# A decoder step with sparse attention and pooling: the pooling means in a queue of their own, and the order of the projections

## The chip, the core and the metric

The kernel runs on one core of a Trainium2 chip. The core has five engines with instruction streams of their own: PE (matrix products and transposes, into PSUM), DVE, ACT and POOL (element-wise work; POOL reads no PSUM here), and SP, which only issues transfers. The metric is the device time of one execution in microseconds, median of three.

## The reference, cut to what matters

One layer of a decoder for 1024 prompt tokens and 8 samples with one token each, 1024 channels. One projection feeds an attention that is cut to 256 keys by an indexer, and a pooling mixer.

```
h = rms_norm(x, norm_w) * (1 + scale) + shift
q, k, v, qi, ki, wi, ga, u, gp = split(h @ w_in)
q, k = rms_norm(q, q_norm_w), rms_norm(k, k_norm_w)          # per head of 64
score = sum over 8 heads of wi * relu(qi . ki)               # causal
sel   = the 256 largest scores of a token
a_out = attention of q over k[sel], v[sel] * silu(ga)        # 8 heads, 2 key heads
d[g]  = mean of u[g] over the last w tokens - u[g]           # w = 2, 4, 8, 16 for groups 0..3
p_out = (d[g] @ w_pool[g]) * pool_scale * silu(gp)
y     = x + gate * (concat(a_out, p_out) @ w_out)
```

For the samples the same runs over 1024 cached keys, values and indexer keys in pages. Returned are y, the new k, v and ki, and the last 15 rows of u for prompt and samples.

## The kernel before, in words

Tokens lie along the free dimension (1032 = 1024 prompt + 8 samples), channels on the 128 partitions. Every product is made of three passes over a split into an upper and a lower part (L514); splits take a copy on ACT and a subtraction on POOL. A projection of 128 columns (`project`, L520) goes through three chunks of 344 tokens (two of 388 for qi), 24 matmuls per partial sum of eight channel blocks, 72 in all.

PE, DVE and ACT run in the order in which the program issues (`manual_schedule`, L424). That order is made by a tick: after every two channel blocks, six matmuls, `project` calls `tick` (L169). It runs what the last chunk left to consume, and then takes one step of each of several queues of generators (`beside`, L155): a queue has a list of generators, of which only the first advances, and a rate; a rate of 1.0 is one step per tick, `SCORE` 0.62 a step in about 1.6 ticks, `TOP` 0.5 one in two. `lag(n)` lets n steps pass without work, and so puts distance between two operations. `drain` (L194) issues what is left in named queues without projections between. POOL's instructions and SP's transfers are ordered by the scheduler, not by the ticks.

First half (`first_order`, L1095): k, the indexer queries qi1 to qi3, gates ga0 to ga2 and v. Beside them run `indexer_keys` and `norm_keys` (queue "prep"; L1043), and in "score" `indexer` (L655), 48 units: matmuls `pi` (L668), a relu on ACT (L670) and a weighted sum on DVE (L677). Then "score" is drained (L1150).

Second half (`order`, L1096): pooling inputs u0 to u3, pooling gates gp0 to gp3, queries q0 to q3 and the gate ga3. Beside them run:

- "prep": `values`, `history`, then `windows(g, u)` (L1180) after each u, and the norms of each q (`take_q`, L1239), one after the other;
- "smp": `sample_indexer` (L868), a pipeline over the eight samples with a period of `IXP` steps (load, transposes `pkin`, copy `kidT`, product `p_ix`, copy `sx`, transposes `p_ixT`, weighing `rx`), then `sample_topk` (L936), a binary search of twelve counts in which DVE makes flags `s_fl` (L968), PE sums them (`p_cnt`, L954) and DVE takes the next step (L972 to L976);
- "top": `topk` (L738): eight halvings of a threshold for blocks 2 to 7, with three sign passes on ACT (L758) and three counts on DVE (L761) each, then `tk_keep`, `tk_d`, `tk_t` (L764 to L768); after these the marking of the largest scores;
- "pool": the pooling product and gate (`take_gp`, L1212), which reads `pooled[g]`;
- "gate" (`gate_rows`, L1493) and "stack" (`stack_k`, `stack_q`), which prepare the output gate and the attention's operands; they start with gp3 and q3, the tenth and the twelfth of 13.

`windows` makes log2(w) shifted sums on POOL (L1187), the mean minus u on DVE (L1192 to L1197), its upper part `pdh` on ACT one step later (L1201), the lower part `pdl` on POOL (L1202), and last it transposes the final rows of u (`put`, L1204) for the output.

The norms of a query group take squares summed on PE (`pqs`), a copy `qs` (L1252), transposes (`pqt`), a reciprocal root that begins with a power on POOL (L253), and DVE's steps, which end in `rq8` and in `qbd` (L1265, L1266), the scaled queries of the samples. The attention over the prompt and the samples' attention (`sample_attention`, L1278) come after the drain at L1539; the samples' first product `p_sl` (L1303) reads `qbd` of all four groups. The output projection ends the kernel.

Large tiles (128 x 1032) come from a pool "rows" of 29 buffers (L98).

Of the kernel before, what the change touches and what calls it, by code (L numbers as in the profile page):

```python
# [21 lines left out]
TOP = 0.5  # L22
SCORE = 0.62
BLOCKS = (3, 4, 2, 5, 7, 6)
ILAG = 1
ILAG0 = 3
QLAG = 3
GLAG = 3
IXP = 4
IXB = 13  # L30
LAG = 5
# [34 lines left out]
def kernel(  # L66
# [40 lines left out]
    def row(name, dt=F32, n=N):  # L107
        return rows.tile([P, n], dt, tag="row", name=name)
# [759 lines left out]
    def sample_indexer():  # L868
# [60 lines left out]

        yield from pipeline(B, IXP, (0, load), (5, turn), (6, copy), (8, dot), (9, copy_x), (IXB, back), (IXB + 1, weigh))  # L930

# [111 lines left out]
    def norm_keys():  # L1043
# [15 lines left out]
        nc.sync.dma_start(k_prompt.rearrange("(b p) d -> p b d", p=P), khat.rearrange("p (b d) -> p b d", d=P))  # L1059
        yield  # L1060
        for g in range(2):
# [118 lines left out]
    def windows(g, u):  # L1180

        w = POOL_WINDOWS[g]
        cur = u
        d = 1
        while d < w:
            nxt = row(f"ps{g}_{d}")
            nc.gpsimd.tensor_tensor(nxt[:, d:S], cur[:, d:S], cur[:, 0:S - d], op=ALU.add)  # L1187
            nc.gpsimd.tensor_copy(nxt[:, 0:d], cur[:, 0:d])
            cur = nxt
            d *= 2  # L1190
            yield from lag(3)
        nc.vector.tensor_tensor(cur[:, S:N], hsum[:, g, :], u[:, S:N], op=ALU.add)  # L1192
        head = small.tile([P, HIST], F32, tag="phead", name=f"ph{g}")[:, 0:w - 1]
        nc.vector.tensor_tensor(head, cur[:, 0:w - 1], inv15[:, 0:w - 1], op=ALU.mult)
        nc.vector.scalar_tensor_tensor(cur[:, w - 1:N], cur[:, w - 1:N], 1.0 / w, u[:, w - 1:N],
                                       op0=ALU.mult, op1=ALU.subtract)
        nc.vector.tensor_tensor(cur[:, 0:w - 1], head, u[:, 0:w - 1], op=ALU.subtract)  # L1197
        hi, lo = row(f"pdh{g}", F32R), row(f"pdl{g}", F32R)
        pooled[g] = (hi, lo)
        yield  # L1200
        nc.scalar.copy(hi, cur)  # L1201
        nc.gpsimd.tensor_tensor(lo, cur, hi.bitcast(F32), op=ALU.subtract)  # L1202
        pt = ps_two(f"put{g}", (HIST + B, P))
        nc.tensor.transpose(pt, u[:, S - HIST:N], ident)  # L1204
        yield
        nc.scalar.copy(up_out[:, g * P:(g + 1) * P], pt)
        if g == 3:
            yield
            nc.sync.dma_start(pool_prompt, up_out[0:HIST, :])
            nc.sync.dma_start(pool_sample[:, HIST - 1, :], up_out[HIST:HIST + B, :])  # L1210

    def take_gp(g):  # L1212
# [26 lines left out]
    def take_q(j):  # L1239
# [3 lines left out]
        def norms():  # L1243
# [276 lines left out]
    for o, name in enumerate(order):  # L1520
        beside("weights", next_weights(len(first_order) + o), 1.0)
        i = int(name[-1])
        kind = name[:-1]
        if name == "gp3":
            beside("gate", gate_rows(), 1.0)
        if name == "q3":
            beside("stack", stack_k(), 1.0)
            beside("stack", stack_q(0), 1.0)
        if kind == "u":
            u = row(f"u{i}")  # L1530
            project(name, CHUNKS, copy_out(u))
            beside("prep", windows(i, u), 1.0)
        elif kind == "gp":
# [3 lines left out]
        else:  # L1537
            project(name, CHUNKS, take_ga(i))
    drain("prep", "pool", "top", "smp", "stack")  # L1539
    in_order.close()  # L1540
# [222 lines left out]
```

## Time and profile before

| | |
|---|---|
| time, median of 3 runs | 644.74 us (644.22 to 647.06) |
| the profiled execution | 646.98 us, span 645.3 us |
| mean clock granted to PE | 0.983 of full speed |
| instructions | 10974 |
| PE / DVE / ACT / POOL busy | 606.9 / 409.8 / 291.5 / 234.1 us |
| HBM read, written | 54.44 MB, 11.10 MB |

Times in the profile are counted from the first instruction of the span. "Idle before" is how long the engine had stood still before an instruction, and behind the arrow stands what released it. PE's first projection of the second half (u0) starts at 184.08 us, its last (ga3) ends at about 385; the attention goes on to about 546, the output projection to the end. The profile counts matmuls as busy with modelled ends, so two that overlap, or one that is followed at once, leave no gap.

### The profile page before, as it was taken

To read this page: it belongs to the slowest core of one execution; us is meant where nothing else is said; L and a number is where in the kernel's file an instruction comes from. 1 tells how busy PE (TensorE), PEld (TensorE's weight loads), DVE (VectorE), ACT (ScalarE), POOL (GpSimd) and SP (SyncE) were. 2 spreads that over 40 slices of the span, in tenths; PEclk is the share of its full clock that TensorE was granted. 3 is DMA by queue.
4 is the path that set the end of the run, shared out by engine and by line. 5 is a ranking of instruction groups with operands and counts; after the bars stand their busy time and mean duration, and the time that the engine had idled before them with its cause. 6 is when DMAs were issued, how large, how long until landed. Compare 5 with 4: busy or idle time off the path is not lost.

```text
span 645.3 us, 10974 instructions
## 1 busy us (share of the span) xinstructions
PE 606.9 (94%) x4197; PEld 500.2 (78%) x4197; DVE 409.8 (64%) x950; ACT 291.5 (45%) x518; POOL 234.1 (36%) x205
## 2 busy tenths in 40 slices
PE   5899998999989987988999998999999999999997
PEld 4678988999979877977989885656675666878876
DVE  4797365736467779997785546565677755454242
ACT  5635444444447865231223445755687545302000
POOL 3202434111267555552633591610445143106000
PEclk9999999999999988997999998999999999999999
DMA  8994115031335122121354350420221036146331
GB/s 302 287 272 95 50 44 152 14 88 54 76 114 161 34 66 56 45 57 44 80 128 156 99 164 27 138 99 34 66 67 34 1 99 218 46 157 205 99 98 68
DMA packets 75292, 66.05 MB, mean 102 GB/s; under 512 B 21828, under 2 KB 63900, under 8 KB 75229
## 3 DMA queue, kind: packets, MB, share of 16 engines
q1 hardware_dynamic: 69731, 50.57, 27.6%
q0 software_dynamic: 3008, 10.49, 5.4%
q10 hardware_dynamic: 2498, 4.27, 1.8%
q8 instruction: 33, 0.54, 0.3%
q14 instruction: 22, 0.18, 0.1%
HBM read 54.44 MB, written 11.10 MB: 102 GB/s over the span
## 4 chain that ended last, share of the span: by engine, by line
PE 73%; DVE 13%; ACT 5%; DMA 3%; SPq 2%; POOL 2%; issue 2%; ACTq 0%; POOLq 0%; DVEq 0%
PE py L1696 14%; PE po L1612 7%; PE pj_q L514 6%; PE pT L1596 6%; PE pl L1575 6%; PE pj_ga L514 6%; PE pj_qi L514 4%; PE pj_gp L514 4%; ACT sg L758 4%; PE pi L668 4%; PE pj_k L514 2%; PE pj_v L514 2%; DVE tk_t L768 2%; PE pj_u L514 2%; PE pj_ki L568 2%
## 5 line engine op out<-in xcount | busy, mean ns | idle before, releaser
L1584 ACT ACTIVATE pr<-pr,mx,rq 128x128 f32<-128x128 f32 (+7 forms) x64 | 55.5, 868 | 17.4 <-DVE mx L1582 17.0
L677 DVE SCALAR_TENSOR_TENSOR sc<-r,wtok,sc 128x512 f32<-128x512 f32 (+5 forms) x42 | 44.0, 1059 | 28.1 <-ACT r L670 26.8
L670 ACT ACTIVATE r<-pi 128x512 f32<-128x512 f32 (+5 forms) x48 | 36.3, 760 | 54.2 <-PE pi L668 41.0
L1612 PE MATMUL po<-pTs,v_sb 128*64 128x256 f32 (+1 forms) x320 | 52.6, 381 | 0.0
L1696 PE MATMUL py<-woh,mh 128*128 128x512 f32 (+1 forms) x136 | 52.1, 383 | 0.0
L1696 PE MATMUL py<-wol,mh 128*128 128x512 f32 (+1 forms) x136 | 51.8, 381 | 0.0
L1696 PE MATMUL py<-woh,ml 128*128 128x512 f32 (+1 forms) x136 | 51.8, 381 | 0.0
L1596 PE MATMUL pT<-ident,pr 128*128 128x128 f32 x288 | 48.8, 283 | 0.1
L1578 DVE CUSTOM_DVE_ANT_0 pr<-pl,amask 128x384 f32<-128x384 f32 (+5 forms) x48 | 42.2, 886 | 9.9 <-PE pl L1575 9.5
L1596 PEld LDWEIGHTS pT<-ident,pr 128*128 128x128 f32 x288 | 32.6, 141 | 17.6 <-issue 15.6
L1716 DVE TENSOR_TENSOR y<-py,gate_p 128x512 f32<-128x512 f32 (+1 forms) x17 | 11.2, 658 | 43.0 <-PE py L1696 42.9
L145 ACT COPY pTs<-pT 128x512 f32<-128x512 f32 x40 | 23.3, 582 | 33.5 <-PE pT L1596 33.5
L514 PE MATMUL pj_u<-hh,wh_u 128*128 128x344 f32 x96 | 32.9, 343 | 1.6 <-ACT r L670 1.6
L514 PE MATMUL pj_gp<-hh,wh_gp 128*128 128x344 f32 x96 | 33.2, 346 | 0.0
L514 PE MATMUL pj_q<-hh,wh_q 128*128 128x344 f32 x96 | 33.0, 344 | 0.0
L147 DVE COPY pTs<-pT 128x512 f32<-128x512 f32 (+1 forms) x40 | 23.3, 582 | 15.0 <-PE pT L1596 12.3
L1440 POOL TENSOR_TENSOR wol<-wo,woh 128x1024 fp32r<-128x1024 f32 x8 | 19.5, 2442 | 36.5 <-ACT woh L1439 29.7
L514 PE MATMUL pj_q<-hl,wh_q 128*128 128x344 f32 x96 | 31.6, 330 | 0.0
L514 PE MATMUL pj_gp<-hl,wh_gp 128*128 128x344 f32 x96 | 31.6, 329 | 0.0
L514 PE MATMUL pj_q<-hh,wl_q 128*128 128x344 f32 x96 | 31.6, 329 | 0.0
L514 PE MATMUL pj_gp<-hh,wl_gp 128*128 128x344 f32 x96 | 31.5, 328 | 0.0
L1612 PEld LDWEIGHTS po<-pTs,v_sb 128*64 128x64 f32 x320 | 18.0, 135 | 17.4 <-issue 9.6
(451 smaller groups left out, 1766.2 us busy)
## 6 DMA issues: line engine op xcount, KB each, us to landing
ada<-in_w_ada_dram SPq DMA_DIRECT2D x16, 512.0 KB, 6.9
x<-in_x_prompt_dram SPq DMA_DIRECT2D x8, 512.0 KB, 5.6
gate<-in_w_ada_dram SPq DMA_DIRECT2D x8, 512.0 KB, 3.5
mix<-mix_dram SPq DMA_DIRECT2D x8, 512.0 KB, 3.1
xr<-in_x_prompt_dram SPq DMA_DIRECT2D x15, 256.0 KB
out_dram<-y ACTq DMA_DIRECT2D x15, 256.0 KB, 3.4
mix_dram<-sga SPq DMA_DIRECT2D x12, 172.0 KB, 5.0
mix_dram<-sgp SPq DMA_DIRECT2D x12, 172.0 KB, 2.7
```

The lines of the kernel that those rows point to most:

```text
L145: nc.scalar.copy(out, in_)
L514: mm(pt[:m, :n], wt[:, k, :m], ht[k][:, c0:c0 + n], start=k == 0 and q == 0, stop=k == KT - 1 and q == 2)
L668: mm(pt[:, c, :n], lhs, kk[:, l0:l0 + n], start=kk is kih, stop=kk is kil)
L670: nc.scalar.activation(r[:, 0:L].rearrange("p (c n) -> p c n", c=nh), pt[:, 0:nh, :n], AF.Relu)
L677: nc.vector.scalar_tensor_tensor(sb[:, 0:L], r[:, 0:L], wtok[:, b, h:h + 1], sb[:, 0:L], op0=ALU.mult, op1=ALU.add)
L758: nc.scalar.activation(junk_tile("sg", tag="junka", bufs=1)[:, :L], score[b], AF.Sign, scale=-1.0, bias=t[:, i:i + 1], accum_out=cnt[:, i: ...
L1575: mm(pt[:, c, :n], qst[j][s][:, b * P:(b + 1) * P], ksst[s][w][:, l0:l0 + n], start=w == 0, stop=w == 1)
L1578: nc.vector.tensor_tensor_reduce(out=pr[:, 0:L].rearrange("p (c n) -> p c n", c=nh), in0=pt[:, 0:nh, :n], in1=amask[b].rearrange("p (c n) ...
L1584: exps.append(lambda: nc.scalar.activation(pr[:, 0:L], pr[:, 0:L], AF.Exp, scale=sc, bias=mx, accum_out=sums[j, m][:, bq, s:s + 1]))
L1596: nc.tensor.transpose(pt[:, s, bq * P:(bq + 1) * P], probs[j, 2 * m + bq, s][:, k * P:(k + 1) * P], ident)
L1612: mm(po[j, m][64 * s:64 * s + 64, 0, q0:], v_sb[:, k, 64 * s:64 * s + 64], pTs[j, m, k][:, s, q0:], start=k == 0, stop=k == nk - 1)
L1696: mm(pt[:, part], a[k][:, bs], w[:, part], start=k == ks[0] and q == 0, stop=k == ks[-1] and q == 2)
```

## The change

`windows` goes from the queue "prep" to a new queue "win", which is created later and so comes after "smp" and "top" in a tick. In it the `put` transposes come first, two steps after the projection, and the means last: two further steps (`WLAG - 1`) behind the three of the last sum, then three steps (`WLAG`) to `pdh` and one to `pdl`; `pooled[g]` is set after that. The order of the projections ends in q2, q3, gp3, ga3 instead of gp3, q2, q3, ga3; "gate" and "stack" start at the same places in the count. `SCORE` is 0.68. In the samples' pipeline `p_ix` comes one step later, `sx` and `p_ixT` two, `rx` two. `norm_keys` waits three steps instead of one before its second transposes. The copy `qs` is on ACT.

```
--- before.py
+++ after.py
@@ -20,14 +20,15 @@
 AHEAD = 1
 HOP = 3
 TOP = 0.5
-SCORE = 0.62
+SCORE = 0.68
 BLOCKS = (3, 4, 2, 5, 7, 6)
 ILAG = 1
 ILAG0 = 3
 QLAG = 3
+WLAG = 3
 GLAG = 3
 IXP = 4
-IXB = 13
+IXB = 15
 LAG = 5
 SMP = 1.2
 
@@ -927,7 +928,7 @@
                 op0=ALU.max, op1=ALU.mult)
             nc.vector.tensor_reduce(out=s_sc[:, 0:8, b], in_=rx[b], axis=AX.X, op=ALU.add)
 
-        yield from pipeline(B, IXP, (0, load), (5, turn), (6, copy), (8, dot), (9, copy_x), (IXB, back), (IXB + 1, weigh))
+        yield from pipeline(B, IXP, (0, load), (5, turn), (6, copy), (9, dot), (11, copy_x), (IXB, back), (IXB + 1, weigh))
 
     steps = const.tile([P, 7, B], F32, name="steps")
     nc.gpsimd.iota(steps, pattern=[[1, 7], [0, B]], base=1, channel_multiplier=0,
@@ -1057,7 +1058,7 @@
             yield
             yield from norm_k(pt, khat[:, g * 512:(g + 1) * 512], 4, P, f"{g}")
         nc.sync.dma_start(k_prompt.rearrange("(b p) d -> p b d", p=P), khat.rearrange("p (b d) -> p b d", d=P))
-        yield
+        yield from lag(3)
         for g in range(2):
             pb = ps_side(f"pkb{g}")
             for i in range(4):
@@ -1093,7 +1094,7 @@
 
 
     first_order = ["k", "qi1", "ga0", "qi2", "ga1", "qi3", "ga2", "v"]
-    order = ["u0", "u1", "u2", "gp0", "u3", "gp1", "q0", "gp2", "q1", "gp3", "q2", "q3", "ga3"]
+    order = ["u0", "u1", "u2", "gp0", "u3", "gp1", "q0", "gp2", "q1", "q2", "q3", "gp3", "ga3"]
     mix_dram = dram.tile([KT, P, N], F32, name="mix_dram")
 
     def cols(name):
@@ -1182,6 +1183,15 @@
         w = POOL_WINDOWS[g]
         cur = u
         d = 1
+        yield from lag(2)
+        pt = ps_two(f"put{g}", (HIST + B, P))
+        nc.tensor.transpose(pt, u[:, S - HIST:N], ident)
+        yield
+        nc.scalar.copy(up_out[:, g * P:(g + 1) * P], pt)
+        if g == 3:
+            yield
+            nc.sync.dma_start(pool_prompt, up_out[0:HIST, :])
+            nc.sync.dma_start(pool_sample[:, HIST - 1, :], up_out[HIST:HIST + B, :])
         while d < w:
             nxt = row(f"ps{g}_{d}")
             nc.gpsimd.tensor_tensor(nxt[:, d:S], cur[:, d:S], cur[:, 0:S - d], op=ALU.add)
@@ -1189,6 +1199,7 @@
             cur = nxt
             d *= 2
             yield from lag(3)
+        yield from lag(WLAG - 1)
         nc.vector.tensor_tensor(cur[:, S:N], hsum[:, g, :], u[:, S:N], op=ALU.add)
         head = small.tile([P, HIST], F32, tag="phead", name=f"ph{g}")[:, 0:w - 1]
         nc.vector.tensor_tensor(head, cur[:, 0:w - 1], inv15[:, 0:w - 1], op=ALU.mult)
@@ -1196,18 +1207,11 @@
                                        op0=ALU.mult, op1=ALU.subtract)
         nc.vector.tensor_tensor(cur[:, 0:w - 1], head, u[:, 0:w - 1], op=ALU.subtract)
         hi, lo = row(f"pdh{g}", F32R), row(f"pdl{g}", F32R)
+        yield from lag(WLAG)
+        nc.scalar.copy(hi, cur)
+        yield
+        nc.gpsimd.tensor_tensor(lo, cur, hi.bitcast(F32), op=ALU.subtract)
         pooled[g] = (hi, lo)
-        yield
-        nc.scalar.copy(hi, cur)
-        nc.gpsimd.tensor_tensor(lo, cur, hi.bitcast(F32), op=ALU.subtract)
-        pt = ps_two(f"put{g}", (HIST + B, P))
-        nc.tensor.transpose(pt, u[:, S - HIST:N], ident)
-        yield
-        nc.scalar.copy(up_out[:, g * P:(g + 1) * P], pt)
-        if g == 3:
-            yield
-            nc.sync.dma_start(pool_prompt, up_out[0:HIST, :])
-            nc.sync.dma_start(pool_sample[:, HIST - 1, :], up_out[HIST:HIST + B, :])
 
     def take_gp(g):
         def finish(ci, c0, n, sg):
@@ -1249,7 +1253,7 @@
                 mm(pq[32 * i:32 * i + 32, g, :], blk[:, 48:80], sq[:, b * P:(b + 1) * P], start=True, stop=True)
             yield
             qs = t2k(f"qs{j}")[:, 0:2 * P].rearrange("p (g t) -> p g t", t=P)
-            nc.vector.tensor_copy(qs, pq)
+            nc.scalar.copy(qs, pq)
             yield from lag(QLAG)
             pr = ps_two(f"pqt{j}", (P, 24, 16))
             for g in range(2):
@@ -1521,22 +1525,22 @@
         beside("weights", next_weights(len(first_order) + o), 1.0)
         i = int(name[-1])
         kind = name[:-1]
+        if name == "q2":
+            beside("gate", gate_rows(), 1.0)
         if name == "gp3":
-            beside("gate", gate_rows(), 1.0)
-        if name == "q3":
             beside("stack", stack_k(), 1.0)
             beside("stack", stack_q(0), 1.0)
         if kind == "u":
             u = row(f"u{i}")
             project(name, CHUNKS, copy_out(u))
-            beside("prep", windows(i, u), 1.0)
+            beside("win", windows(i, u), 1.0)
         elif kind == "gp":
             project(name, CHUNKS, take_gp(i))
         elif kind == "q":
             project(name, CHUNKS, take_q(i))
         else:
             project(name, CHUNKS, take_ga(i))
-    drain("prep", "pool", "top", "smp", "stack")
+    drain("win", "prep", "pool", "top", "smp", "stack")
     in_order.close()
     banks.close()
     psb = banks.enter_context(tc.tile_pool(name="psb2", bufs=2, space=PSUM))
```

## Rows read from the trace of the kernel before

**Rows 1.** The page: span, and busy time of each engine (share, instructions).
```profile
span 645.3 us, 10974 instructions
...
PE 606.9 (94%) x4197; PEld 500.2 (78%) x4197; DVE 409.8 (64%) x950; ACT 291.5 (45%) x518; POOL 234.1 (36%) x205
```

**Rows 2.** Busy us (instructions) of PE, PEld, DVE, ACT, POOL by stretch; then PEclk, DMA.
```profile
195.00:246.00 51.00, 46.24 (x329) 41.69 (x328) 39.86 (x98) 38.34 (x71) 32.45 (x29) 0.97 0.27 75
246.00:293.00 47.00, 38.93 (x263) 37.38 (x262) 45.63 (x78) 13.91 (x27) 27.61 (x19) 0.95 0.22 54
293.00:385.00 92.00, 91.86 (x702) 83.94 (x703) 60.40 (x143) 29.41 (x53) 47.56 (x26) 0.97 0.41 115
```

**Rows 3.** Waits of PE, whole span: who, for whom; us, times, longest.
```profile
PE p_cnt L954 <- DVE s_fl L968: 5.5, 2, 4.2
PE p_sl L1303 <- DVE qbd L1266: 3.9, 1, 3.9
PE put L1204 <- ACT pt L1220: 2.7, 1, 2.7
PE p_ix L911 <- ACT kidT L905: 2.6, 3, 1.8
PE p_ixT L920 <- DVE rx L925: 2.2, 3, 1.7
...
PE pkb L1065 <- POOL khat L1040: 1.5, 1, 1.5
```

**Rows 4.** Chain that ended last, 195 to 246: share by line.
```profile
by line: ACT sg L758 45.4%; DVE tk_t L768 20.3%; issue 8.9%; DVE tk_keep L764 5.3%; DVE ps L1195 4.8%; DVE junk L761 4.1%; PE pj_u L514 2.5%; ACT pdh L1201 2.1%; DVE tk_d L766 1.7%; ACT u L1021 1.3%; ACT kidT L905 1.0%; PE pkin L901 0.9%; D
```

**Rows 5.** The same chain, 246 to 293.
```profile
by line: DVE sc L778 16.7%; DVE fl L773 11.1%; DVE s_H L976 10.8%; DVE s_cand L966 10.4%; DVE s_fl L968 7.2%; DVE tk_top L792 6.6%; DVE ps L1195 5.0%; DVE tk_need L781 4.9%; DVE s_lo L707 4.8%; DVE s_sc L940 4.6%; issue 3.1%; DVE s_d L975 2
```

**Rows 6.** Timeline, end of first half: start, us, engine, line, operation, [idle before].
```profile
174.24 0.45 PE L668 MATMUL pi<-kih,qis 128*128 128x320 f32 x2
...
178.04 0.74 PE L668 MATMUL pi<-kih,qis 128*128 128x512 f32 x2
...
184.08 0.43 PE L514 MATMUL pj_u<-hh,wh_u 128*128 128x344 f32 x1 [1.65 <-ACT r L670]
```

**Rows 7.** Waits of ACT between 195 and 293.
```profile
ACT pdh L1201 <- DVE ps L1197: 5.4, 2, 3.6
```

**Rows 8.** Lines 768, 976, 1195 on DVE: ns minimum/median/maximum, first and last start.
```profile
L768 DVE TENSOR_TENSOR tk_t<-tk_t,tk_d x8: 166/194/6221, 201.2 to 246.5; 128x6 f32<-128x6 f32 x8
...
L976 DVE SCALAR_TENSOR_TENSOR s_H<-s_d,s_H x6: 168/1262/2336, 264.0 to 302.6; 128x8 f32<-128x8 f32 x6
...
L1195 DVE SCALAR_TENSOR_TENSOR ps<-ps,u x4: 1220/1229/1233, 203.2 to 284.4; 128x1031 f32<-128x1031 f32 x1, 128x1029 f32<-128x1029 f32 x1, 128x1025 f32<-128x1025 f32 x1, 128x1017 f32<-128x1017 f32 x1
```

**Rows 9.** Timeline around 236, DVE and POOL.
```profile
236.23 6.22 DVE L768 TENSOR_TENSOR tk_t<-tk_t,tk_d 128x6 f32<-128x6 f32 x1
...
236.35 1.90 POOL L1187 TENSOR_TENSOR ps<-u 128x1023 f32<-128x1023 f32 x1
...
240.54 1.88 POOL L1187 TENSOR_TENSOR ps<-ps 128x1022 f32<-128x1022 f32 x1
```

**Rows 10.** Timeline of ACT: a copy of 128 by 256.
```profile
356.01 0.37 ACT L1509 COPY ev_g<-pa_g 128x256 f32<-128x256 f32 x1 [3.63 <-PE pa_g L1506]
```

**Rows 11.** Busy time in two equal stretches, columns as in rows 2.
```profile
292.00:298.80 6.80, 5.66 (x27) 5.42 (x28) 5.52 (x16) 0.00 (x0) 0.55 (x1) 0.50 0.40 105
298.80:305.60 6.80, 6.80 (x63) 6.27 (x63) 4.21 (x8) 2.29 (x4) 2.39 (x1) 1.00 0.00 0
```

**Rows 12.** Timeline, start of the attention.
```profile
384.83 4.17 POOL L253 TENSOR_TENSOR y<-ms,nhalf 128x24 f32<-128x24 f32 x1
...
389.03 0.18 DVE L255 TENSOR_TENSOR yt<-y 128x24 f32<-128x24 f32 x1 [5.60 <-POOL y L253]
...
390.25 0.38 PE L1303 MATMUL p_sl<-knT,qbd 128*32 128x128 f32 x2 [3.87 <-DVE qbd L1266]
...
394.45 0.27 PE L1596 MATMUL pT<-ident,pr 128*128 128x128 f32 x1
```

More of the change, by code (lines that the diff above doesn't have):

```diff
@@ L22 @@
 TOP = 0.5
-SCORE = 0.62
+SCORE = 0.68
 BLOCKS = (3, 4, 2, 5, 7, 6)
@@ L928, in weigh @@
             nc.vector.tensor_reduce(out=s_sc[:, 0:8, b], in_=rx[b], axis=AX.X, op=ALU.add)
-        yield from pipeline(B, IXP, (0, load), (5, turn), (6, copy), (8, dot), (9, copy_x), (IXB, back), (IXB + 1, weigh))
+        yield from pipeline(B, IXP, (0, load), (5, turn), (6, copy), (9, dot), (11, copy_x), (IXB, back), (IXB + 1, weigh))
     steps = const.tile([P, 7, B], F32, name="steps")
@@ L1059, in norm_keys @@
         nc.sync.dma_start(k_prompt.rearrange("(b p) d -> p b d", p=P), khat.rearrange("p (b d) -> p b d", d=P))
-        yield
+        yield from lag(3)
         for g in range(2):
@@ L1184, in windows @@
         d = 1
[L1185 to L1202, printed above, removed]
+        yield from lag(2)
         pt = ps_two(f"put{g}", (HIST + B, P))
@@ L1210, in windows @@
             nc.sync.dma_start(pool_sample[:, HIST - 1, :], up_out[HIST:HIST + B, :])
+        while d < w:
+            nxt = row(f"ps{g}_{d}")
+            nc.gpsimd.tensor_tensor(nxt[:, d:S], cur[:, d:S], cur[:, 0:S - d], op=ALU.add)
+            nc.gpsimd.tensor_copy(nxt[:, 0:d], cur[:, 0:d])
+            cur = nxt
+            d *= 2
+            yield from lag(3)
+        yield from lag(WLAG - 1)
+        nc.vector.tensor_tensor(cur[:, S:N], hsum[:, g, :], u[:, S:N], op=ALU.add)
+        head = small.tile([P, HIST], F32, tag="phead", name=f"ph{g}")[:, 0:w - 1]
+        nc.vector.tensor_tensor(head, cur[:, 0:w - 1], inv15[:, 0:w - 1], op=ALU.mult)
+        nc.vector.scalar_tensor_tensor(cur[:, w - 1:N], cur[:, w - 1:N], 1.0 / w, u[:, w - 1:N],
+                                       op0=ALU.mult, op1=ALU.subtract)
+        nc.vector.tensor_tensor(cur[:, 0:w - 1], head, u[:, 0:w - 1], op=ALU.subtract)
+        hi, lo = row(f"pdh{g}", F32R), row(f"pdl{g}", F32R)
+        yield from lag(WLAG)
+        nc.scalar.copy(hi, cur)
+        yield
+        nc.gpsimd.tensor_tensor(lo, cur, hi.bitcast(F32), op=ALU.subtract)
+        pooled[g] = (hi, lo)
     def take_gp(g):
@@ L1523 @@
         kind = name[:-1]
+        if name == "q2":
+            beside("gate", gate_rows(), 1.0)
         if name == "gp3":
-            beside("gate", gate_rows(), 1.0)
-        if name == "q3":
             beside("stack", stack_k(), 1.0)
@@ L1538 @@
             project(name, CHUNKS, take_ga(i))
-    drain("prep", "pool", "top", "smp", "stack")
+    drain("win", "prep", "pool", "top", "smp", "stack")
     in_order.close()
```

9 lines of the change are left out of this document (5 added, 4 removed).

## Prediction

> **What bounds the kernel now.** I read four views in this order. First the page's engine shares: PE is busy 94% of a span of 645.3 us [rows 1], so on the whole only a wait of PE can be won. Then the busy times by stretch [rows 2]: from 293 to 385 PE is busy 91.86 of 92 us, while between 195 and 293 it is busy 46.24 of 51 and 38.93 of 47 us; in the last of these DVE has 45.63 of 47. So the second projection phase is not bound by PE until 293. Third, PE's waits [rows 3]: counting of the samples' search (p_cnt) 5.5 us, the samples' first dot product (p_sl) 3.9, the transposes of the pooling input (put) 2.7, p_ix 2.6, p_ixT 2.2, the keys' second transpose (pkb) 1.5. The change touches every one of these. Fourth, the chain of waits, which tells which of them set the end. From 195 to 246 it runs over ACT's sign passes (45.4%) and DVE's threshold update tk_t (20.3%) [rows 4]; from 246 to 293 every line named is DVE's [rows 5]. There PE's waits for put, p_ix and p_ixT are effects: removing them alone only lets PE reach the p_cnt wait earlier. What counts is how early DVE issues its fifth search step, and how late PE asks for it.
>
> I count steps (one step is six projection matmuls and one call of the queues) from the start of u0; the phase has 13 x 12 = 156.
>
> **Part by part.** The sum is made against the profiled execution, 646.98 us (span 645.3 and 1.7 around it). The median shown is 644.74, 2.2 lower; I carry the difference over to it.
>
> *Keys' lag, one step to three.* The pkb transposes wait 1.5 us for the last khat product on POOL [rows 3]. Two more steps are twelve projection matmuls, more than the wait; what hides it is the running projection. If POOL were later still, nothing is lost. Bounds 0 to 1.7, I take -1.5.
>
> *SCORE 0.62 to 0.68.* Working the queue's accumulator through the 84 steps of the first half leaves nine of 48 score units to the drain at 0.62 and four at 0.68. The drain runs from 174.24 to 184.08, 9.8 us; its last four units begin at 178.04, so 6.0 us remain [rows 6]. The five moved units took 3.8 us, but they still need their 16 matmuls among the projections, which fill most of that. The end of the drain, PE idle 1.65 us behind ACT's last relu [rows 6], stays: it is the alternation of relu and weighing. Bounds 0 and -3.8 plus up to 1.6 lost to a new wait of pi behind a relu (a wait of pkb's size); I take -0.8.
>
> *Means in their own queue, with distances.* Means g0 to g3 move from steps 16, 31, 46, 73 to 21, 37, 56, 79, the upper halves (pdh) from 17, 32, 47, 74 to 24, 40, 59, 82; no operation is added. Today pdh stands one step behind its means, and ACT stands still for it 5.4 us, with sign passes and sgp copies queued behind [rows 7]. That goes. In 195 to 246 the chain holds 4.8% ps, 4.1% junk, 2.1% pdh and 5.3% keep [rows 4], 8.3 of 51 us, put there mostly because means g0 and g1 stand ahead of DVE's counting. Behind the counting they still cost: the means are 1.23 us each [rows 8] plus three tiny operations, and lengthen the halving in which they now stand, some 1.2 us each; pdh0 now stands between two sign passes, 1 us. Net -4.9 at best. But a larger share is of another kind: tk_t holds 20.3% of the chain [rows 4], 10.4 us, where eight at their least, 166 ns, are 1.3; the longest took 6221 ns [rows 8], beside back-to-back POOL operations [rows 9]. The POOL operations all stay, so this price is drawn anew. I take -1.8, near the middle between -4.9 and a loss of one more such case, +6.0.
>
> The Trainium skill (SBUF — State Buffer, Who interferes with whom) says that a DVE instruction with two SBUF inputs contends with a GpSimd instruction that reads SBUF, and that the second to issue is blocked until the first is finished. The trace agrees in kind, 6.22 us for a sum of 128 by 6 [rows 9]; by the rule the moves alone take no blocking away, which speaks against this part, and its own result stands among the rivals.
>
> From 246 to the fifth p_cnt: means g3 (1.7 us with its small operations) falls behind that point. So does its lower half pdl3, beside which the longest s_H update took 2336 ns against 168 [rows 8]; pdl1 comes in instead, at up to the same price. p_cnt H4 moves from step 80 to 82: a step of the PE-bound stretch is 92/76 = 1.2 us [rows 2], so 2.4 us of cover, less one more top-k operation in DVE's order, about 1. Sum -1.7 -1.4 and the swap at 0: -3.0 (bounds -5.3 and +3). The copies qs go from DVE to ACT, four of 128 by 256, 0.37 us on ACT [rows 10]; ACT is busy 13.91 of 47 us and 29.41 of 92 [rows 2], so nothing.
>
> *Clock.* After the p_cnt wait PE ran at half clock for 6.8 us: 27 matmuls at 0.50 against 63 in the next 6.8 us at 1.00 [rows 11]. 36 matmuls at 6.8/63 = 0.11 us are 3.9 us, inside the stretch that PE bounds from 293 on. With the p_cnt wait 3 us shorter I think it an even case that this fall is shorter or gone: -1.5 (bounds 0 and -3.9).
>
> *put and samples' spacing.* put needs the projection's last copy, which ACT makes behind three sign passes. At its new place, two to three steps after it, put1 may wait up to one halving's share of sign passes (45.4% of 51 us over eight, 2.9 us [rows 4]) less the steps between; put2 waits 2.7 today [rows 3]. p_ix has one step more behind kidT, which covers 1.2 us of its longest wait, 1.8 [rows 3]; p_ixT keeps its four steps. As PE is not the bound there: 0 (bounds -1 and +2).
>
> *Order: q2, q3 ahead of gp3.* Matmuls are the same, SP loads the same pieces in another order, the gate starts at the same step. q3's reciprocal root (POOL, 4.17 us) starts at 384.83 today; DVE is idle 5.60 us for it, and the p_sl dot products stand 3.87 us behind qbd [rows 12]. With q3 24 steps earlier in order, its root is issued at step 144 instead of 154 and its DVE part at 150 of 156, some 6 steps or 7 us ahead of need. What is late next: DVE can take the first logits from 386.4, where PE's wait began, instead of 390.25, and from there the first probability transposes come 4.2 us later (394.45 today) [rows 12]; so -3.9, less POOL. Into POOL's last steps come three gate products of gp3 beside the stacking, and qst must be complete before the first logits; if it is late by as much as one root takes, 4.17 us, nothing is won. I take -3.2 (bounds 0 and -5.6: the wait and half of the 3.4 us that a fall of the clock, as at 292, would cost at half the length of rows 11). The rows pool holds 29 tiles; pdh3 and pdl3 now live beside qp2, qp3 and the stacked keys, and my count reaches 29 to 30, so gate_s waits for a score row freed by the masks two steps before its use: 0 to +1, taken as 0.
>
> Sum: -1.5 -0.8 -1.8 -3.0 -1.5 -3.2 = -11.8, so 635.2 for an execution like the profiled one and 633 by the median.
>
> **Rivals.**
> 1. The middle gives its gain back: DVE's order is as late as before, waits only change their name (put to p_cnt). Then keys, drain and end remain, -5.5: 639.2. For it: DVE is the chain for 47 us [rows 5] and loses one operation only. Against: the two steps at p_cnt are certain.
> 2. The end is not won either: POOL places q3's root behind the stacking, or qst is late, and the wait of 3.9 us moves from qbd to the first logits. With the middle given back: -2.3, 642.4.
> 3. Slower: pile-ups on the halvings. pdl0, the first sums of g1 and the weights' lower half now become ready together, and so do pdl1 and the sums of g2; each pile of three POOL operations that meets tk_t or tk_keep costs what the one at 236.23 cost, 6.05 us over its minimum [rows 9]. With keys, drain and end won (-5.5) and two piles more, +12.1: 651.3. It decides from 8.7 us of added stretching. The Trainium skill's rule on the two SBUF inputs (SBUF — State Buffer, Who interferes with whom) would bring it about. For it: tk_t has a median of only 194 ns [rows 8], so most halvings are still clear and could be hit. Against: g2's sums now have a chance to fall behind the halvings.
> 4. The middle and the clock at their good side (-4.9, -5.3, -3.9), keys and drain as above, the end's 3.9 in full: -20.3, 624.4.
>
> **How the numbers follow.** Forecast 633 (own range 627 to 639): 0.55. Rival 1: 0.21. Rival 2: 0.11. Rival 3: 0.08. Rival 4: 0.05. About 0.5%, 3.2 us, is what a measurement of this kernel can tell from no change: faster is below 641.5, slower above 648. Of rival 1 some 0.17 lies below, the other 0.04 and rival 2 lie between, rival 3 above. Faster 0.77, same 0.15, slower 0.08. The range 625 to 645 leaves out rival 3, half of rival 4 and the far end of rival 2.
>
> **What would show it.** Right: pkb without a wait; pj_u starting 2 us earlier; no wait of ACT for ps; p_sl without a wait for qbd and the first pT about 11 us earlier than 394.45; PE's wait for p_cnt at 3 us or below. Wrong: DVE's fifth s_fl as late as today against the start of u0 (rival 1), tk_t or tk_keep with more than one value over 4 us (rival 3), pl waiting for qst (rival 2). The forecast fails if the stretch between the start of u0 and the fifth p_cnt is not shorter than today's 109 us (184.08 to about 293) [rows 2, 6].

## The result, and the profile after

The changed kernel takes 635.83 us (median of 4 runs, 634.29 to 636.24), against 645.15 us for the kernel before beside it: a ratio of 0.985, 95% interval 0.982 to 0.987. The forecast was 633, its own range 627 to 639. The profiled execution took 634.29 us, with a span of 632.6 against 645.3: it is the fastest of its runs, and the profiled one of before (646.98) is near its slowest, so the two profiles lie 12.7 us apart and the medians 9.3. A profile shows one execution, and executions of one kernel lie up to 7 us apart (experiment 4), so a difference of a few microseconds between two profiles is safe only where several kernels show it.

To see where the time went, each span is cut at the same five events of the timeline. The entries are differences of start times (for the flags, of the end); "keep" is the last `tk_keep` of the eight halvings, "flags" the fifth `s_fl` of the search, "count" the fifth group of `p_cnt`.

| stretch, us | before | after | difference | predicted |
|---|---|---|---|---|
| span start to first matmul of k | 60.52 | 59.21 | -1.31 | 0 |
| first of k to first of u0 | 123.56 | 123.55 | -0.01 | -2.3 |
| first of u0 to keep | 61.98 | 54.67 | -7.31 | -1.8 |
| keep to fifth count | 47.08 | 50.81 | +3.73 | -3.0 |
| fifth count to last matmul of ga3 | 91.60 | 88.84 | -2.76 | -1.5 |
| there to the first pT | 9.71 | 4.35 | -5.36 | -3.2 |
| first pT to the end | 250.83 | 251.16 | +0.33 | 0 |

The first line is not the change's: PE waits there for the transfers of x, which arrive differently in every execution (the experiments below have 58.5 to 60.8). So the total is right for partly wrong reasons. The first half gave nothing, the halvings four times their term, after which half as much was lost before the fifth count, and the end came out near its bound.

The page of the kernel after, span and busy times as in [rows 1]:

```profile
span 632.6 us, 10965 instructions
...
PE 603.4 (95%) x4197; PEld 497.7 (79%) x4197; DVE 391.7 (62%) x946; ACT 292.0 (46%) x522; POOL 237.7 (38%) x205
```

Busy times by stretch of the kernel after, columns as in [rows 2]: the halvings, the stretch from there to the fifth flags, the rest of the projections.

```profile
193.70:237.40 43.70, 42.36 (x320) 38.55 (x318) 30.58 (x97) 37.17 (x70) 24.09 (x23) 1.00 0.33 87
237.40:286.30 48.90, 41.21 (x272) 40.12 (x271) 46.35 (x77) 12.96 (x25) 35.78 (x25) 0.93 0.27 64
286.30:377.10 90.80, 89.79 (x703) 80.97 (x702) 52.98 (x148) 32.50 (x60) 51.94 (x26) 1.00 0.35 99
```

Against [rows 2], DVE does the halvings in 30.58 us of work instead of 39.86 (97 instructions and 98); but in the second stretch it is as full as before (46.35 of 48.9 against 45.63 of 47) and POOL is busy 35.78 instead of 27.61. The three sums of g2 have moved out of the first stretch into the second; the four of g3 were in the second already.

PE's waits in the kernel after, columns as in [rows 3]:

```profile
PE p_cnt L955 <- DVE s_fl L969: 5.7, 3, 3.3
PE pi L669 <- ACT r L671: 3.1, 2, 2.9
PE put L1188 <- DVE rx L926: 1.9, 1, 1.9
...
PE p_ix L912 <- DVE sx L917: 1.1, 1, 1.1
PE ppo L1221 <- DVE qss L1265: 1.0, 1, 1.0
```

The waits for pkb, p_ixT and p_sl are gone, p_ix and put are shorter. The sum for p_cnt is where it was, but not the place: the fifth count, which waited 4.2 us, waits no more, and now the second waits 3.3. ppo is new, and so is a wait of 2.9 us at one go for pi in the first half.

ACT's wait for the means between 193 and 288 us (as in [rows 7]), in the kernel after:

```profile
ACT pdh L1211 <- DVE ps L1208: 5.8, 1, 5.8
```

The wait that the distances were to cover is still there, once, at 258 us (before: two, 5.4 us in all). Within the halvings it is gone, where it was 1.8 us before. DVE's lines 769 and 977 in the kernel after, as in [rows 8], where they are 768 and 976:

```profile
L769 DVE TENSOR_TENSOR tk_t<-tk_t,tk_d x8: 166/166/167, 199.8 to 237.8; 128x6 f32<-128x6 f32 x8
...
L977 DVE SCALAR_TENSOR_TENSOR s_H<-s_d,s_H x6: 166/476/2208, 259.9 to 296.0; 128x8 f32<-128x8 f32 x6
```

`tk_t` now takes its least time in all eight halvings; of the 6.22 us in [rows 9] nothing is left. What remains of that kind in the halvings is one `tk_keep` and one `tk_d`, both beside a sum `ps` on POOL. Timeline of the kernel after (start, us, engine, line):

```profile
204.50 2.39 DVE L765 TENSOR_TENSOR tk_keep<-tk_cnt,tk_least 128x6 f32<-128x6 f32 x1 [2.29 <-ACT sg L759]
204.94 1.91 POOL L1197 TENSOR_TENSOR ps<-u 128x1023 f32<-128x1023 f32 x1
```

The start of the attention in the kernel after, as in [rows 12]:

```profile
367.63 4.17 POOL L254 TENSOR_TENSOR y<-ms,nhalf 128x24 f32<-128x24 f32 x1 [1.37 <-DVE ms L253]
371.83 0.90 DVE L256 TENSOR_TENSOR yt<-y 128x24 f32<-128x24 f32 x1 [4.34 <-POOL y L254]
373.46 0.17 DVE L1270 TENSOR_TENSOR qbd<-qp,qrs 64x8 f32<-64x8 f32 x1
374.30 5.35 POOL L1475 TENSOR_TENSOR qst<-qp,qst 64x512 fp32r<-64x512 f32 x4
...
378.61 0.41 PE L1307 MATMUL p_sl<-knT,qbd 128*32 128x128 f32 x2
...
381.43 0.27 PE L1600 MATMUL pT<-ident,pr 128*128 128x128 f32 x1
```

q3's root still costs DVE 4.34 us of standing still, but that ends six microseconds before the first logits (378.05); `qbd` is ready 5 us before `p_sl` reads it.

### The profile page after: what moved, and what is told of

It reads as the page before. It is cut to its first block, busy times and chain, and to the rows that moved or that the text cites. A ratio compares the mean times of both kernels' runs of the same rounds, so it can differ in the third digit from the quotient of the medians.

```text
span 632.6 us, 10965 instructions
## 1 busy us (share of the span) xinstructions
PE 603.4 (95%) x4197; PEld 497.7 (79%) x4197; DVE 391.7 (62%) x946; ACT 292.0 (46%) x522; POOL 237.7 (38%) x205
## 4 chain that ended last, share of the span: by engine, by line
PE 70%; DVE 10%; ACT 5%; SPq 4%; POOL 3%; issue 3%; DMA 3%; POOLq 0%; ACTq 0%; DVEq 0%
PE py L1700 14%; PE po L1616 7%; PE pj_q L515 7%; PE pT L1600 6%; PE pj_ga L515 6%; PE pl L1579 6%; PE pj_gp L515 4%; PE pi L669 4%; PE pj_qi L515 3%; ACT sg L759 3%; SPq L328 2%; PE pj_k L515 2%; PE pj_v L515 2%; SPq L281 2%; DVE sc L779 1%
## 5 line engine op out<-in xcount | busy, mean ns | idle before, releaser
L1588 ACT ACTIVATE pr<-pr,mx,rq 128x128 f32<-128x128 f32 (+7 forms) x64 | 55.4, 866 | 12.3 <-DVE mx L1586 11.8
L515 PE MATMUL pj_ga<-hh,wh_ga 128*128 128x344 f32 x96 | 31.7, 330 | 0.0
L515 PE MATMUL pj_ga<-hh,wl_ga 128*128 128x344 f32 x96 | 31.3, 326 | 0.0
```

Source lines behind the costliest of these rows:

```text
L515: mm(pt[:m, :n], wt[:, k, :m], ht[k][:, c0:c0 + n], start=k == 0 and q == 0, stop=k == KT - 1 and q == 2)
L1588: exps.append(lambda: nc.scalar.activation(pr[:, 0:L], pr[:, 0:L], AF.Exp, scale=sc, bias=mx, accum_out=sums[j, m][:, bq, s:s + 1]))
```

## The experiments

First each part of the change alone, added to the kernel before; the four together are the whole change. The ratio is to the kernel before, timed beside it on the same chip. This table, from the timelines, is what the readings rest on (us; the stretches as above, u0 to the fifth flags and to the last ga3 both from the first matmul of u0):

| kernel | ratio (95% interval) | k to u0 | u0 to keep | u0 to fifth flags | u0 to last ga3 | ga3 to pT |
|---|---|---|---|---|---|---|
| before | 1 | 123.56 | 61.98 | 109.00 | 200.66 | 9.71 |
| order alone | 0.993 (0.991 to 0.995) | 123.55 | 62.38 | 108.82 | 200.99 | 4.59 |
| means' queue alone | 0.991 (0.989 to 0.994) | 123.58 | 54.66 | 101.42 | 191.64 | 10.31 |
| SCORE and keys alone | 1.000 (0.999 to 1.002) | 123.55 | 57.57 | 106.61 | 198.16 | 9.77 |
| spacing and qs alone | 0.996 (0.993 to 0.998) | 123.59 | 57.58 | 106.31 | 194.96 | 10.30 |
| after (all four) | 0.985 (0.982 to 0.987) | 123.55 | 54.67 | 103.57 | 194.32 | 4.35 |
| order and means' queue | 0.982 (0.981 to 0.984) | 123.54 | 54.65 | 101.39 | 192.30 | 4.62 |
| after, sums a memset | 0.969 (0.968 to 0.970) | 123.50 | 51.99 | 93.31 | 184.28 | 4.34 |
| after, norms spread | 0.984 (0.982 to 0.987) | 118.84 | 57.72 | 106.49 | 198.77 | 4.33 |
| order, queue, SCORE, keys, norms spread | 0.977 (0.974 to 0.979) | 118.81 | 54.71 | 101.42 | 192.39 | 4.62 |

**1. The order alone.**

```
-    order = [..., "q1", "gp3", "q2", "q3", "ga3"]
+    order = [..., "q1", "q2", "q3", "gp3", "ga3"]
```
(with the start of "gate" at q2 and of "stack" at gp3, as in the change)

> The kernel before with the order of the projections alone (q2, q3 ahead of gp3, gate and stack at the same counts). Theory: all that the changed kernel wins behind its last projection, 5.4 us between the last matmul of ga3 and the first probability transpose, comes from this order, and nothing before it; time 5 to 6 us below before, the wait of 3.87 us of the samples' first product gone and the first pT 9.7 us after the last pj_ga as before becomes about 4.3. Rival: the wait goes only together with the means' earlier and spaced places, since q3's root then meets less POOL work; then this kernel wins 2 us or less, and a wait of 2 us or more stands before the first product or the first logits.

639.61 us against 644.39. Every stretch up to the last ga3 is as before within 0.4 us, and the one behind it is 5.1 us shorter. Timeline of this kernel:

```profile
381.58 5.34 POOL L1471 TENSOR_TENSOR qst<-qp,qst 64x512 fp32r<-64x512 f32 x4
...
384.26 0.30 PE L1575 MATMUL pl<-ks0h,qst 128*128 128x128 f32 x1 [0.46 <-POOL qst L1471]
...
384.83 0.41 PE L1303 MATMUL p_sl<-knT,qbd 128*32 128x128 f32 x2
...
387.63 0.27 PE L1596 MATMUL pT<-ident,pr 128*128 128x128 f32 x1
```

`p_sl` waits for nothing and `qst` is late by 0.46 us only: the theory holds, and the prediction's fear that POOL's stacking would eat the gain (its rival 2) does not.

**2. The means' queue alone.** The edits of `windows` (`put` first, the distances, `pooled[g]` last) with this:

```
-            beside("prep", windows(i, u), 1.0)
+            beside("win", windows(i, u), 1.0)
```

> The kernel before with the means' queue alone (own queue, put first, the distances). Theory: it brings the halvings' 7 us (last keep of the top-k about 8 us earlier against the start of u0) and, as the counts of the search give most of it back, some 4 to 6 us of the whole; the small DVE updates tk_t and tk_d hold at most two values over 2 us in place of the three or more of before. Rival: the middle's gain belongs to the samples' spacing and to qs on ACT, which take waits out of the same stretch; then this kernel is within 2 us of before, and the fifth count ends as late after the start of u0 as before (about 109 us).

638.33 us. The halvings are 7.3 us shorter, and here the gain is not given back: the fifth flags come 7.6 us earlier against u0 and the last ga3 9.0 us, more than in the whole change. At the end 0.6 us are lost. Between the medians the time falls by 6.1. In the halvings two small updates over 2 us remain, as expected; that the counts would give most of it back was wrong.

**3. SCORE and the keys' distance alone.**

```
-SCORE = 0.62
+SCORE = 0.68
...
-        yield
+        yield from lag(3)
         for g in range(2):
             pb = ps_side(f"pkb{g}")
```

> The kernel before with SCORE 0.68 and the keys' three steps alone. Theory: the wait of 1.5 us for pkb goes and the drain is four units instead of nine, but the score units that now stand earlier meet DVE's blocked key norms, so PE waits some 2.9 us for a relu at about 95 us and loses clock after it; start of u0 within 0.7 us of before when counted from the first ki matmul, time within 1 us of before. Rival (the prediction's terms): 2.3 us faster, and the wait at 95 us stays at 1.4 us; it would then be a matter of the other parts.

644.63 us, ratio 1.000; k to u0 is 123.55 us. PE's wait for `pi` is 3.1 us, as in the kernel after, and its clock falls to half behind it. Busy times of this kernel in two equal stretches, columns as in [rows 2]:

```profile
98.50:101.90 3.40, 3.40 (x13) 3.31 (x12) 1.93 (x3) 1.24 (x2) 2.48 (x1) 0.51 0.10 32
101.90:105.30 3.40, 3.40 (x23) 3.38 (x22) 3.02 (x6) 1.27 (x2) 1.73 (x2) 0.99 0.00 0
```

13 matmuls instead of 23 in 3.4 us. The gain that the prediction counted is there, and it is given back in the same half.

The run held a surprise: the halvings, which begin 10 us behind the last thing that was edited, became 4.4 us shorter. Timeline of this kernel at the place of [rows 9]:

```profile
236.35 1.89 POOL L1187 TENSOR_TENSOR ps<-u 128x1023 f32<-128x1023 f32 x1 [0.35 <-ACT u L1021]
236.37 1.89 DVE L768 TENSOR_TENSOR tk_t<-tk_t,tk_d 128x6 f32<-128x6 f32 x1
238.20 2.40 POOL L297 TENSOR_TENSOR wl_u<-wr_u,wh_u 128x1024 fp32r<-128x1024 f32 x1
238.36 1.15 ACT L758 ACTIVATE sg<-sc,tk_t 128x1024 bf16<-128x1024 f32 x1 [0.66 <-DVE tk_t L768]
```

In [rows 9] the same `tk_t` is recorded from 236.23, 0.12 us ahead of the sum on POOL, and ends only with the third POOL operation, after 6.22 us; here it is recorded 0.02 us behind the sum and ends with that one, after 1.89. Its place in DVE's order is the same. The long case is not one odd execution: in experiment 1, recorded 0.56 us ahead of the sum, the same `tk_t` took 6.67 us. So a shift of a tenth of a microsecond between DVE and POOL goes with 4.3 us of this one update, and an edit elsewhere can throw this die again. What is won there need not reach the end: 2.5 of the 4.4 us are left at the last ga3, the attention of this profile is 1.1 us longer, and the median is that of the kernel before.

**4. The spacing and qs alone.**

```
-IXB = 13
+IXB = 15
...
-(8, dot), (9, copy_x)
+(9, dot), (11, copy_x)
...
-            nc.vector.tensor_copy(qs, pq)
+            nc.scalar.copy(qs, pq)
```

> The kernel before with the samples' spacing (dot, copy, transposes and weighing one to two steps later) and the copy qs on ACT alone. Theory (the prediction): PE is not the bound where p_ix and p_ixT wait, so nothing is won: time within 1 us of before, the waits of p_ix and p_ixT (2.6 and 2.2 us) shorter, those of p_cnt as much longer. Rival: the spacing makes up for a part of the middle's gain, 2 to 4 us, as DVE's sx no longer stands in order behind a late p_ix.

640.92 us: 3.5 won, where prediction and theory said none. The halvings are 4.4 us shorter, again by the one `tk_t` (1891 ns here as in experiment 3). A second gain is the spacing's own: the search stands two steps later in PE's order, so that 12 projection matmuls more are done by the fifth count (492 instead of 480). The rival named the right size for another reason.

The four parts alone add up to 2.0% (0.7, 0.9, 0 and 0.4), the whole change has 1.5%, which the intervals hardly tell apart. The profiles do: from u0 to the last ga3 the parts alone have +0.3, -9.0, -2.5 and -5.7, together -16.9, and the whole has -6.3. They win the same time, not time beside each other. So the next runs leave parts out.

**5. Order and means' queue, without the rest.** Experiments 1 and 2 together.

> The kernel before with the order of the projections and the means' queue together, without the spacing, qs on ACT, SCORE 0.68 and the keys' steps. Theory: the two parts act in different stretches and add (4.8 and 6.1 us below the 644.4 that the kernel before takes beside them), and the spacing adds nothing to them, since it won its 3.5 us alone by the same stretching of small DVE updates that the means' queue already cures: 633.5, with the middle at 9 us less than before against the start of u0, and so about 2 us below the changed kernel as one profile has it, or equal to it. Rival: the spacing's 3.5 us are its own (two steps more of cover for the search's counts); then this kernel is 3 us slower than the changed one, 639.

632.53 us: the stretches of the two parts alone come out again, and nothing is missing without the spacing. Against the kernel after the last ga3 comes 2.0 us earlier after u0, and PE has no wait for ppo. The two intervals overlap (0.981 to 0.984 and 0.982 to 0.987), so the whole time says only that spacing, SCORE and keys bring nothing on top of these two.

**6. POOL's sums replaced.** The kernel after; the shifted sums, and so the pooling means, are left out.

```
-            nc.gpsimd.tensor_tensor(nxt[:, d:S], cur[:, d:S], cur[:, 0:S - d], op=ALU.add)
-            nc.gpsimd.tensor_copy(nxt[:, 0:d], cur[:, 0:d])
+            nc.gpsimd.memset(nxt[:, 0:S], 1.0)
```

> The changed kernel with POOL's shifted sums replaced by a memset of the same rows, which reads nothing (the means are left out by it). Theory: DVE's small operations are held until the end of a POOL operation that reads SBUF; without the sums the two stretched updates in the halvings (2.39 and 2.57 us) are gone, as are most of those of the search beside ps (about 6 of 8 us), the last keep comes 4 us earlier against the start of u0, and the fifth flags some 3 to 6 us; the time falls by 2 to 5 us. Rival: the stretching comes from POOL's writes or from any work on POOL; then the stretched updates stay beside the memsets and the time stays within 1 us, or falls only by what the memset is shorter than a sum (1.9 us).

624.33 us, ratio 0.969. Timeline, and line 769, of this kernel, at the place where the kernel after has its 2.39 us:

```profile
204.55 0.17 DVE L765 TENSOR_TENSOR tk_keep<-tk_cnt,tk_least 128x6 f32<-128x6 f32 x1 [2.29 <-ACT sg L759]
204.82 0.17 DVE L767 SCALAR_TENSOR_TENSOR tk_d<-tk_keep,tk_step 128x6 f32<-128x6 f32 x1
204.97 0.97 POOL L1197 MEMSET ps<- 128x1024 f32 x1
205.02 0.17 DVE L769 TENSOR_TENSOR tk_t<-tk_t,tk_d 128x6 f32<-128x6 f32 x1
```

`tk_t` runs inside the memset at its least time, 0.17 us, where beside a sum it took 1.82 to 6.22. So what holds `tk_t` is not POOL's being busy, nor its writing, but an operation that reads. And the busy times, columns as in [rows 2]:

```profile
193.80:234.90 41.10, 41.10 (x312) 37.55 (x312) 26.36 (x98) 37.16 (x70) 22.33 (x19) 1.00 0.34 92
234.90:276.20 41.30, 39.68 (x279) 38.60 (x279) 38.78 (x77) 13.07 (x24) 25.65 (x18) 1.00 0.32 76
```

PE is never idle in the halvings, and from keep to the fifth flags DVE does the same 77 instructions in 38.78 us instead of 46.35. Those 7.6 us are the whole shortening of this stretch, and PE's wait for p_cnt falls from 5.7 to 0.8 us. The gain against the kernel after, 10 us, is twice the most that was expected: the updates of the search that are held stay about as many as before (two `s_H` of 2.2 and 2.3 us and an `s_cand` of 2.3 us remain, beside other POOL operations that read), but larger operations, as the marking `sc` of block 6 with 2.77 us at 244.86 in the kernel after, had been held by the sums too; the same `sc` takes 1.15 us here. This is an upper bound of the price, as a memset is half as long as a sum (0.97 us against 1.9) and the means no longer wait for sums either.

**7. More distance in the keys' norms.** The kernel after, with

```
         rest = rstd_of(rs, ss, 2 * nblk, 64, parts=parts)
-        yield
+        yield from lag(3)
         rest()
```

> The changed kernel with three steps instead of one between the power on POOL and DVE's following steps in the keys' norms. Theory: PE's wait of 2.9 us for a relu at 92 to 95 us stands behind DVE, which waits in order for the power and is then held by the weights' lower half on POOL; with two steps more the weighing goes first, the wait falls below 1 us, the half clock after it is gone, and u0 starts 3 to 4.5 us earlier against the first matmul of k (123.55 us now); time 3 to 4 us below the changed kernel. Rival: DVE is only held by the weights' lower half (2.3 us), which it meets two steps later as well; then the wait moves or stays, the start of u0 within 0.5 us.

What it is about, in the timeline of the kernel after:

```profile
88.66 1.64 POOL L240 TENSOR_TENSOR y<-ms,nhalf 128x8 f32<-128x8 f32 x1 [5.69 <-DVE ms L239]
90.26 2.38 POOL L298 TENSOR_TENSOR wl_qi<-wr_qi,wh_qi 128x1024 fp32r<-128x1024 f32 x1
90.33 2.34 DVE L243 TENSOR_TENSOR yt<-y 128x8 f32<-128x8 f32 x1 [1.75 <-POOL y L240]
...
93.71 0.61 DVE L676 TENSOR_SCALAR sc<-r,wtok 128x768 f32<-128x768 f32 x1
...
94.44 1.02 ACT L671 ACTIVATE r<-pi 128x1024 f32<-128x1024 f32 x1 [6.02 <-DVE sc L676]
```

DVE waits in order for the power, is then held by the weights' lower half for 2.34 us, and only at 93.71 weighs the score unit whose buffer ACT needs; ACT has stood still 6.02 us, and PE waits for it. With the longer distance the `yt` is held just as long (2.35 us at 91.60), but the weighing is ahead of it: PE's wait for `pi` is 0.2 us from 59 to 178 us, and k to u0 takes 118.84 us, 4.7 less. The rival falls. Yet the time is 634.74, not 3 to 4 us lower. Busy times of this kernel around the start of u0 (178.57), as in [rows 2]:

```profile
172.30:179.00 6.70, 4.79 (x23) 3.44 (x22) 4.97 (x5) 4.65 (x6) 1.54 (x3) 1.00 0.00 0
179.00:185.90 6.90, 6.90 (x27) 6.33 (x27) 2.20 (x8) 1.82 (x3) 5.00 (x5) 0.51 0.44 122
185.90:192.70 6.80, 6.80 (x46) 6.41 (x46) 3.21 (x16) 1.96 (x5) 5.59 (x11) 1.00 0.97 303
```

Behind the drain, PE runs at half clock: 27 matmuls in 6.9 us against 46 in the next 6.8. That puts the last keep 3.05 us back against u0, and another 1.4 us are lost by the last ga3.

**8. The best of it.** Order, means' queue, SCORE 0.68, the keys' steps and the longer distance in their norms, without spacing and qs on ACT.

> Order, means' queue, SCORE 0.68, the keys' steps and the longer distance in the keys' norms, without the spacing and qs on ACT. If the theories of the other two hold (nothing lost without the spacing, 3 to 4 us won in the first half) this is the fastest: 629 to 631. If the spacing's gain is its own, 633 to 635; if the norms' distance wins nothing either, as the kernel with order and queue alone.

628.20 us (627.7 to 631.55), ratio 0.977 (0.974 to 0.979): the fastest that computes everything, and below the kernel after by both intervals. Its stretches are those of experiment 7 up to u0 and of experiment 5 from there on. At the same place as above its clock did not fall:

```profile
172.30:179.00 6.70, 4.80 (x25) 3.51 (x23) 5.41 (x6) 3.82 (x5) 2.50 (x3) 1.00 0.00 0
179.00:185.90 6.90, 6.90 (x46) 6.27 (x45) 3.67 (x16) 2.71 (x5) 6.10 (x6) 1.00 0.69 201
```

PE had been idle as long in both kernels (1.9 us of 6.7), and one was set to half clock, the other not. What decides between them stays open. It may differ from execution to execution: one of five of experiment 7 took 631.70 us, 2.8 less than the next, and one of five here 631.55, 2.7 more, but only one of each was profiled.

## Why the prediction was right, and where it was not

*Keys' lag and SCORE, -1.5 and -0.8: measured 0 together.* The wait for pkb went and the drain is shorter: its first product starts at 176.8 instead of 174.24 [rows 6], with the same 1.7 us before u0.

```profile
176.83 0.62 PE L669 MATMUL pi<-kih,qis 128*128 128x512 f32 x2
...
182.76 0.43 PE L515 MATMUL pj_u<-hh,wh_u 128*128 128x344 f32 x1 [1.71 <-ACT r L671]
```

The prediction allowed up to 1.6 us for a new wait of pi behind a relu, but took it as an end of the range and let the term stand at a gain. What failed is the cover: it took the projections as what hides the longer distance and the moved units, and did not follow DVE, which weighs the units and is at that point held in the norms. The longest wait for pi grew from 1.4 to 2.9 us and drew a fall of the clock with it; experiment 7 shows that with DVE's order mended the half is 4.7 us shorter.

*Halvings, -1.8: measured -7.3.* The term was mis-sized, and its working shows how: the chain gave 10.4 us to tk_t [rows 4], and the text expected that price to be "drawn anew", with the mean of a gain and one more loss. The draw was a good one, and for the sum that is luck. The wait of ACT that the term named was 1.8 us within the halvings. Held updates in the halvings (durations above the lower quartile of their kind, summed) fell from 11.4 us to 4.8, which is 6.6 of the 7.3. The queue's distances thus gave less than where POOL's sums now fall. It is no accident of one execution: in the kernel after and in experiments 2, 5 and 8, all with the means' queue, u0 to keep takes 54.65 to 54.72 us, with the same two updates held. Experiments 3 and 4 threw the same die with edits that have nothing to do with the means and won 4.4 each within the halvings; experiment 6 shows what is left to win there, another 2.7.

*To the fifth count, -3.0: measured +3.7, of which 1.9 are 12 projection matmuls (0.16 us apart) that now stand ahead of it.* The two steps of cover were thus real. The other 1.9 are DVE's. From keep to the fifth flags it took 47.0 us before, 46.8 and 46.7 in experiments 2 and 5, which have the means' queue without the spacing, and 48.9 in the kernel after. Two steps failed. The first is "the swap at 0": the means of g3 left this stretch, 1.7 us as counted, and the queue still brought only 0.3. The exchange was not pdl3 against pdl1 alone. The three sums of g2 came in from the halvings as well, and the six markings `sc` take 3.8 us more, in sum 11.6 us in experiment 5 against 7.8 before: one is 1.5 us longer beside a sum of g2, two are 2.8 longer beside pdl1 and pdl2, and one is shorter. Line 778 of the kernel before and line 779 of experiment 5:

```profile
L778 DVE SCALAR_TENSOR_TENSOR sc<-fl,tk_d,sc x6: 883/1218/2101, 249.7 to 274.7; 128x1024 f32<-128x1024 bf16 x1, 128x896 f32<-128x896 bf16 x1, 128x768 f32<-128x768 bf16 x1, 128x640 f32<-128x640 bf16 x1
L779 DVE SCALAR_TENSOR_TENSOR sc<-fl,tk_d,sc x6: 1019/1838/2866, 239.9 to 271.5; 128x1024 f32<-128x1024 bf16 x1, 128x896 f32<-128x896 bf16 x1, 128x768 f32<-128x768 bf16 x1, 128x640 f32<-128x640 bf16 x1
```

Updates of the search are held for less there, and DVE waits 0.7 us longer for the last keep; of the 1.7 us that the means gave, 0.3 are left. The second step is the spacing at 0: in the kernel after DVE stands still 1.27 us for a transpose `p_ixT`, and two operations have come ahead of the fifth flags, a `tk_top` of 0.8 us and an `sx` of 0.3, as in experiment 4; together 2.4 us, about the 2.2 by which it is slower than experiment 5. Timeline of the kernel after:

```profile
244.28 0.23 DVE L926 SCALAR_TENSOR_TENSOR rx<-p_ixT,wsb 128x64 f32<-128x64 f32 x1 [1.27 <-PE p_ixT L921]
```

Up to the fifth count the two terms together were -4.8 and came to -3.6.

The Trainium skill (SBUF — State Buffer, Who interferes with whom) says that a DVE instruction with two SBUF inputs contends with a GpSimd instruction that reads SBUF, not with one that only writes. Experiment 6 agrees on both halves: 0.17 us within a memset, 1.82 and more beside a sum. The prediction cited the first half and made a loss of it (rival 3, 651.3, at 0.08). What it cited besides, that the second to issue is blocked, does not fit [rows 9]: `tk_t` is recorded 0.12 us ahead of the sum and is still the one held. The same rule could have been read the other way: whoever knows which operations are held can ask where POOL's will now fall, and the sums' later steps were in the diff.

*Clock, -1.5: measured -2.8 behind the fifth count*, of which 1.9 are the matmuls done earlier and not the clock, while a new wait for ppo takes 1.0. The term was right in kind: the half clock at 292 [rows 11] is gone, and in experiments 2 and 5, which have as many projection matmuls behind the fifth count as the kernel before (456), this stretch is 2.6 and 1.9 us shorter at a granted clock of 1.00, against 0.97. Another half clock stands at 263, where DVE sets the pace and not PE.

```profile
263.40:270.20 6.80, 5.46 (x27) 5.46 (x27) 6.59 (x12) 0.55 (x1) 6.72 (x5) 0.50 0.01 2
270.20:277.00 6.80, 6.80 (x52) 6.67 (x50) 6.59 (x9) 1.01 (x2) 6.06 (x6) 1.00 0.07 19
```

New is 1.0 us for ppo behind DVE's `qss`. It is absent in experiments 1 to 5 and 8 and present in 6 and 7, so it takes the spacing or qs together with another part; which, wasn't tried.

*put and spacing, 0: near 0 beside the other parts, wrong alone.* The spacing with qs on ACT alone won 3.5 us, and without it nothing is lost (experiment 5). Its waits were effects, as the prediction said; what it won alone was the draw on tk_t and the cover of two steps, and in the whole the cover is paid for by DVE's 2.2 us above.

*Order, -3.2: measured -5.4, alone -5.1.* The mechanism was right. The size is the 3.87 us of the wait and about the upper bound of the clock's half behind it: in the 3.4 us from p_sl on the granted clock was 0.61 before and is 1.00 in the kernel after (378.6 to 382.0); POOL's stacking, for which the prediction held 0.7 back, was late by 0.46 us alone, and in the whole the first logits wait 0.20 us, for a gate.

The terms from u0 to pT summed to -9.5 and came to -11.7. With the first half's -2.3 missing, the span's start luckier by 1.3 and the rest +0.3, -12.7 in the profiles stands beside -11.8 predicted. Rival 1, the middle given back, happened in part: of 7.3 us won in the halvings, 1.9 were lost by the fifth flags. Of the five signs that the prediction named for itself two came: pkb without a wait, and p_sl without one and pT 13 us earlier. The other three did not: u0 no earlier against the first matmul of k, ACT still waiting for a sum, and p_cnt at 5.7 us. Still, the time came out near, by luck in part: the one gain that was in none of them, DVE's held updates, was larger than what failed.

## What to carry to other kernels

Where DVE's chain of small updates runs beside POOL's large operations, look in the timeline for small DVE instructions of many times their least length that end with a POOL instruction, sum them, and count that sum as a price that any edit can change in either direction, by more than the edit itself is worth. Follow a moved unit through every engine that must consume it, not only the one on which it was late. When an edit takes a wait away, try its parts alone and left out: here two parts of four gave as much as all four, and two steps more of distance in the keys' norms, with SCORE and the keys' steps, brought another 4.3 us on top of the two.

## What the runs showed of the hardware

- Which of DVE's operations are held beside a sum on POOL: a count with one SBUF input that also writes its accumulator was not (0.61 to 0.88 us in all 24 of the kernel after, with sums of 1.9 us beside some), while a copy with one input of two bytes was, 1.93 us for 128 by 72. The Trainium skill (same page and section) has both: a copy whose operands meet certain conditions can enter a mode that shares the port, the form that writes its accumulator cannot. Timeline of the kernel after:

```profile
247.76 1.89 POOL L1197 TENSOR_TENSOR ps<-ps 128x1020 f32<-128x1020 f32 x1
247.77 1.93 DVE L704 COPY s_hi<-s_sc 128x72 int16<-128x72 int16 x1
249.60 0.93 POOL L1226 TENSOR_TENSOR sgp<-sgp,pt 128x344 f32<-128x344 f32 x1
249.62 0.97 DVE L705 COPY s_lo<-s_sc 128x72 uint16<-128x72 uint16 x1
```

- A held operation may be held by one POOL operation or by three in a row: 1.89 us in experiment 3 and 6.22 before for the same `tk_t`, with starts that differ by 0.14 us against the first of them.
- The same stretch of idle before u0 (PE busy 4.79 and 4.80 of 6.7 us at full clock) was followed by half clock in one kernel and by full clock in another.
